# Raw weights of an attention loop on GpSimd's DMA queue, masks on VectorE, partial products in place

## The chip, the cores and the metric

The kernel runs on one core of one Trainium2 chip. The metric is device microseconds of one execution; the time of a kernel is the median of several executions. A core has five engines that run their own instruction streams in order: TensorE (PE, with its weight loads as PEld), VectorE (DVE), ScalarE (ACT), GpSimd (POOL) and SyncE (SP), which here does nothing but issue DMAs. An instruction waits on semaphores for what it needs, and whatever is behind it on its engine waits with it.

## The reference

One inference step of a two-layer encoder trunk, for 512 prompt tokens and 8 x 16 sample tokens (640 tokens, five blocks of 128) that share the weights, all in fp32. Layer 0 is a gated MLP with a spatial mixer; layer 1, where the change lies, is forgetting attention with 16 heads of 128:

```python
proj = h @ w_in                       # (640, 1024) @ (1024, 4 * 2048 + 16): q, k, v, z, forget logits
logf = log_sigmoid(proj[..., 4 * E:] + b_f)
cT = cumsum(logf, axis=1)             # per head
s = einsum('bqhd,bkhd->bhqk', q, k) * scale + cT[..., q] - cT[..., k]
s = where(key_pos <= query_pos, s, -inf)
o = einsum('bhqk,bkhd->bqhd', softmax(s), v)
out = (o * silu(z)) @ w_out
```

Prompt tokens attend to the prompt. Sample tokens attend to 256 cached keys and values of their own sequence (`cache_fox_k`, `cache_fox_v`, `cache_fox_logf`) and to their own 16 new ones. Keys, values and logf of the new tokens are outputs too. After each layer follow a norm, the residual, and a gated embedding.

## The kernel before

**Products with seven multiplications.** fp32 products are made of three fp32r products: each operand is split into a high and a low part (`split`, lines 276 to 283: ACT writes the high part, DVE the low one), and `mm3` (lines 260 to 264) issues high x high, high x low, low x high. In the attention loop a 1024 x 256 panel of `w_in` times the 640 tokens is done in seven block products instead of eight, Strassen-like: `seven_left` yields left operands that are sums and differences of weight blocks, `seven_products` (line 533) multiplies them with sums of token blocks and adds the results up. The weight sums are made by POOL, four additions of 128 x 512 for each panel (`left_operands`, line 203), out of the raw weights into the buffer `SF` (traced as sff). The results' partial sums are `m1`, `u2` and `u3`, three buffers `partial` of 128 x 320 (`HT` = 320 columns, half of the tokens): m1 is written after product 0 (ACT, line 548), u2 after product 1 (DVE, line 550), u3 after product 2 (line 552); they end in the four results `into(i, j)` at products 3 to 6 (line 539, called by `total`).

**Raw weights.** The weights arrive as units of 512 KB; a panel is two units, a pair. From unit `S2` on (64 units, to `S3`) they belong to the attention layer, as in_fox_w_in. `raw_of` says where a unit lies: three slots of 1024 columns (`RAW`), taken in turn. `fetch` issues loads in the order of the units, all on SP's queue through `dma` (line 121). `prefetch` works ahead of TensorE: for each item (a pair's four groups of left operands, j = 0 to 3) it lays down the sums, the split and then `fetch(u + 4)`, at j = 3 `fetch(u + 5)`. With three slots, the second unit of the next pair lies where the first unit of the present one was, so its load waits for POOL's sums and the first split; the unit after that waits for the split of j = 3.

**The attention loop.** Heads go in pairs, p = 0 to 7. In turn p the projections z(p), v(p+1), k(p+1), q(p+1), four panels, are the steps on TensorE (`project`), and `interleave` lays attention pieces of heads 2p and 2p+1 between them, each at a due time in steps' units (a product's k-step counts 0.441, so a panel 12.35). For each prompt head: `setup` splits q and k, and for four query blocks `scores(i)`, `turn(i)` (transposes of the probabilities) and `values(i)`. `scores` first adds the causal mask to the diagonal part of the bias row: w0 is the head's cumulative log-forget row spread over the partitions (`load_w0`, a DMA from c_sc), w1 = w0 + causal for 128 columns (POOL, line 958, one buffer), and DVE subtracts w0 and w1 from the scores while it takes the maximum (lines 968 and 971). For the sample tokens there are two groups of four sequences per pair of heads: `masks` loads the bias `Wc` (from cs_sc) and adds a mask to its last 16 columns (POOL, line 1032) ten units before the scores.

**The queues.** All DMAs of the loop are issued by SP in one order: cached keys (`load_k`, four DMAs each, then turned by DVE at line 1016 out of one buffer), cached values (`load_v`), raw weights, bias rows, stores of new keys (`project_k`: DVE turns them into the buffer `o_vk`, line 904, and 16 DMAs out<-R store them) and of new values, and of y (y_sc). The order of each engine's instructions is planned by a simulation of the program when it is built; the program's order and due times are its input. After the loop, z(7) and the tail of layer 1 follow, in which the last heads' attention lies between the steps of the output product.

Of the kernel before, what the change touches and what calls it, by code (L numbers as in the profile page):

```python
# [20 lines left out]
ALU = mybir.AluOpType  # L21
# [3 lines left out]
P = 128  # L25
# [32 lines left out]
def hybrid_trunk(tc, x_prompt, x_sample, ck, cv, clf, p_prompt, p_sample, norm_pre, norm_post,  # L58
# [58 lines left out]

    behind = {}

    def dma(out, in_):  # L120
        behind["sp"] = nc.sync.dma_start(out=out, in_=in_)  # L121

    @contextmanager
    def queued(*engines):
# [56 lines left out]
    def raw_of(i):  # L181
        if S0 <= i < S1:
            z = (i - S0 + 1) % 4
            if z == NRAW:
                return r1(o_X, 1024)
        else:
            z = i % NRAW if i < S0 else (i + 1) % NRAW
        return RAW[:, z * 1024:z * 1024 + 1024]

    def fetch(upto):  # L190
        while state["raw"] < min(upto, len(units)):
            ap, k = units[state["raw"]]
            dma(raw_of(state["raw"]).rearrange("p (k n) -> p k n", k=k), ap)
            state["raw"] += 1

    def left_operands(i, j):
# [9 lines left out]
    def prefetch(upto, i0=0):  # L206

        while len(place) < min(upto, len(items)):
            i = len(place)
            u, j = items[i]  # L210
            taken = {z for k in range(i0, i) for z in place[k]}
            step = 1 if j == 0 else 2
            free = [z for z in range(0, 2 * (NW - (u in few)), step) if not taken & set(range(z, z + step))]
            if not free:
                return
            z = min(free, key=lambda z: max(last_use[z:z + step]))
            place.append(range(z, z + step))
            last_use[z:z + step] = [i] * step
            fetch(u + 1 if j is None else u + 2)
            o, n = z * 1024, step * 512  # L220
            hi, lo = W[:, o:o + n], W[:, o + n:o + 2 * n]
            if u in joined:
                k = units[u][1]
                hi, lo = (W[:, o:o + 2 * n].rearrange("p (k z n) -> p z k n", z=2, k=k)[:, z] for z in range(2))
                split(hi, lo, raw_of(u).rearrange("p (k n) -> p k n", k=k))
            elif j is None:
                split(hi, lo, raw_of(u))
            else:
                split(*((x.rearrange("p (k n) -> p k n", k=4) for x in (hi, lo)) if j == 0 else (hi, lo)), left_operands(u, j),
                      scale if u in scaled else None)  # L230
                if u > S0:
                    fetch(u + 4 + (u > S1 and j == 3))

    def weights(n):

# [290 lines left out]
        return r1(g // 4 * 2560, 2560).rearrange("p (t n) -> p t n", t=NT)[:, :, (g % 4) * P:(g % 4 + 1) * P]  # L526

    partial = [r1(o_sum + z * HT, HT) for z in range(3)]
    HALF = (slice(0, HT), slice(HT, TOK))

    UZ = (0, 1, 2, 3)

    def seven_products(into, done):

        m1, u2, u3 = partial
        rights = (quarter(0, 0), right_sum(1), quarter(0, 1), right_sum(0), quarter(1, 1), quarter(1, 0), right_sum(2))

        def total(i, j, a, b):
            behind["dve"] = nc.vector.tensor_tensor(out=into(i, j), in0=a, in1=b, op=ALU.add)  # L539
            done(i, j, into(i, j))  # L540

        for n, (w, right) in enumerate(zip(seven_left(), rights)):
            o = bank(UZ)[:, :HT]
            for k in range(4):
                mm3(o, (w[0][:, k], w[1][:, k]), (right[0][:, k], right[1][:, k]), k == 0, k == 3)
                yield 0.441
            if n == 0:
                nc.scalar.activation(out=m1, in_=o, func=AF.Copy)
            elif n == 1:
                nc.vector.tensor_tensor(out=u2, in0=m1, in1=o, op=ALU.add)  # L550
            elif n == 2:
                nc.vector.tensor_tensor(out=u3, in0=u2, in1=o, op=ALU.add)  # L552
            elif n == 3:
                total(1, 1, u3, o)
                nc.vector.tensor_tensor(out=u2, in0=u2, in1=o, op=ALU.add)  # L555
            elif n == 4:
                total(0, 1, u2, o)
            elif n == 5:
                total(0, 0, m1, o)
            else:  # L560
                total(1, 0, u3, o)
# [31 lines left out]
    spatial_loads(1)  # L593
    for g in range(0, 16, 2):
        for part, finish in ((0, finish_u), (1, finish_z)):
            run(seven_products(lambda i, j: uv_of(g + i)[part][:, HALF[j]], lambda i, j, c: finish(g, i, j, c)))
            if part == 0:

                with queued("act", "dve"):
                    spatial_weights(g)  # L600
                    spatial_weights(g + 1)
        if g < 6:

            with queued("act", "dve"):
                layer_norm_panel(1 + g // 2)
        for i in range(2):
            gate_spatial(g + i)
# [139 lines left out]
    SF = pool2.tile([P, 2560], F32, name="sff")  # L747

    o_KT, o_K, o_V, o_q, o_k, o_vk = 0, 2176, 3200, 5248, 6528, 7808
    o_u, o_P, o_PT, o_v, o_qp = 9088, 9728, 10752, 11776, 14336  # L750
    o_Ws, o_Ps, o_PTs, o_W0, o_z = 14848, 15120, 15520, 15904, 16480
    assert o_z + 2 * TOK <= N_R1
    partial = [SF[:, 2048:2048 + HT], r1(o_u, HT), r1(o_u + HT, HT)]


    o = 0
# [163 lines left out]
    def project_z(p):  # L920

        def done(i, j, c):
            th = r1(o_vk + ring("th", (0, 1)) * HT, HT)
            nc.scalar.activation(out=th, in_=c, func=AF.Tanh, scale=0.5)
            nc.vector.scalar_tensor_tensor(out=c, in0=th, scalar=1.0, in1=c, op0=ALU.add, op1=ALU.mult)

        yield from seven_products(lambda i, j: both(o_z, i)[:, HALF[j]], done)

    def project(*parts):
        for part in parts:  # L930
            yield from part

    W0 = [r1(o_W0, 512), tri]
    w1_at = lambda: SF[:, 2368:2368 + P]

    def load_w0(h):
        dma(W0[h % 2], c_sc[h].partition_broadcast(P))

    def prompt_pieces(h):

        p, hh = h // 2, h % 2
        q, k, v = q_of(h), k_of(h), v_of(p)
        w0 = W0[hh]
        zs = (NW - 1) * 2048
        qh, ql, kh, kl = (W[:, zs + z * 512:zs + (z + 1) * 512] for z in range(4))
        O = PB[7]
# [6 lines left out]
        def scores(i):  # L953
            n = (i + 1) * P
            d = slice(i * P, n)
            S = bank(ATT)
            w1 = w1_at()
            nc.gpsimd.tensor_tensor(out=w1, in0=w0[:, d], in1=causal, op=ALU.add)
            if i:
                mm3(S[:, :n], (qh[:, d], ql[:, d]), (kh[:, :n], kl[:, :n]), True, True)  # L960
            else:
                nc.tensor.matmul(S[:, :n], q[:, d], k[:, :n], start=True, stop=True)
            pr = prs[i] = r1(o_P + ring("P", (0, 1)) * 512, 512)
            m = small()
            init = -3e38
            if i:
                m0 = small()
                nc.vector.tensor_tensor_reduce(out=pr[:, :i * P], in0=S[:, :i * P], in1=w0[:, :i * P], scale=1.0, scalar=init,
                                               op0=ALU.subtract, op1=ALU.max, accum_out=m0)
                init = m0  # L970
            nc.vector.tensor_tensor_reduce(out=pr[:, d], in0=S[:, d], in1=w1, scale=1.0, scalar=init,
                                           op0=ALU.subtract, op1=ALU.max, accum_out=m)
            nm, sm = small(), small()
            nc.vector.tensor_scalar(out=nm, in0=m, scalar1=-1.0, scalar2=None, op0=ALU.mult)  # L974
            nc.scalar.activation(out=pr[:, :n], in_=pr[:, :n], func=AF.Exp, bias=nm, accum_out=sm)  # L975
            ri = small()
            nc.vector.reciprocal(out=ri, in_=sm)
            nc.vector.tensor_scalar(out=pr[:, :n], in0=pr[:, :n], scalar1=ri, scalar2=None, op0=ALU.mult)
# [43 lines left out]
    def sample_pieces(p, bg):  # L1022
# [6 lines left out]

        def masks():  # L1030
            dma(Wc, cs_sc[16 * p + 8 * bg:16 * p + 8 * bg + 8].unsqueeze(1).broadcast_to([8, TS, 272]))
            nc.gpsimd.tensor_tensor(out=Wc[:, PAST:], in0=Wc[:, PAST:], in1=CST[:, C_M16:C_M16 + TS], op=ALU.add)

        def scores():
            S = bank(ATT)
            for hh in range(2):
                for bl in range(4):
                    nc.tensor.matmul(S[32 * bl:32 * bl + 32, :272], qpads[:, hh, 4 * bg + bl].rearrange("p h q -> p (h q)"),
                                     kt[:, hh, bl], start=(hh == 0), stop=(hh == 1))
# [71 lines left out]
    def attention_pieces(p, step, s1):  # L1111
# [6 lines left out]
            pieces += prompt_times(2 * p + hh, t0 + 4 * step * hh, step)  # L1118
        if p < 7:
            pieces += [(s0 + 12.1, lambda: load_k(p + 1, 0, 0)), (s1 + 13.5, lambda: load_v(p + 1, 0)),  # L1120
                       (t0 + 4 * step, lambda: load_w0(2 * p + 2))]
        return pieces

    def next_keys(p, t, t_new):
# [4 lines left out]
    sums = []  # L1129

    def sums_of_h():
        sums.append(right_operands((13056, 14336, 15616, o_P, o_V)))

    interleave(project_v0(), [(0.0, forget_logits), (0.1, sums_of_h), (6.0, log_forget)])
    split(*quarter(0, 1), sums[0])
# [15 lines left out]
    pool2.release()  # L1151
    pool2, R2 = second("r2c", F32)
    load_y(range(2, 14))
    w1_at = lambda: r2(9840, P)
    ATT = (5, 6)
    o_junk = r2(9200, 512)
    tail(1, y_again, (0, 1, 2, 3, 4), [(t - now, g) for t, g in pieces if t > now])
# [32 lines left out]
```

## Time and profile before

| | us |
|---|---|
| median of 3 runs (1409.69 to 1413.42) | 1412.28 |
| the profiled execution | 1413.11 |
| its span on the core | 1411.3 |
| busy in it: PE / DVE / ACT / POOL | 1316.6 / 946.7 / 586.6 / 354.9 |

The span runs through layer 0 (its seven-product loop and tail) to about 545 us, the start of layer 1 to about 600, the attention loop from 601 to 1195, and the tail of layer 1. In a row of the profile stand a line of the kernel, an engine, an operation, what it writes and reads by the names of the buffers (R is the large buffer `R1`, A and tbf token operands, W split weights, pb a PSUM bank, SML small columns, CST constants), how often, busy us and the mean ns of one, then the engine's idle time just before them and what ended it. `SPq` is SP's sequencer issuing DMAs. PEclk is the clock that TensorE was granted.

### The profile page before, as it was taken

The numbers are of one execution on the slowest core, as the hardware profiler recorded it, in microseconds if no ns is written. First come the engines' busy times: TensorE is split into PE (matmuls) and PEld (weight loads), VectorE is DVE, ScalarE is ACT, GpSimd is POOL, SyncE is SP. The second block draws the span as 40 slices with busy tenths as digits, with TensorE's granted clock in tenths as the row PEclk, the third lists the DMA queues.
The fourth block names the chain that finished last, engine by engine and source line by source line (L and its number), as shares of the span: only waits on it lengthen the run. The fifth ranks groups of instructions, "written<-read, shape, count | busy, mean of one in ns | idle before, by whom it ended". The sixth has DMA issues, their size and how long they took to land.

```text
span 1411.3 us, 21215 instructions
## 1 busy us (share of the span) xinstructions
PE 1316.6 (93%) x7877; PEld 1169.1 (83%) x7877; DVE 946.7 (67%) x1815; ACT 586.6 (42%) x1061; POOL 354.9 (25%) x332
## 2 busy tenths in 40 slices
PE   9999999999999998999788899798887989999998
PEld 6888999999888887878677798687776978888887
DVE  6745999999434659877556767656665676745553
ACT  4424554445353434343333344333323344545332
POOL 1014444550000003344313334333232332100000
PEclk9999999999999999999899999898998999999999
DMA  6432333323342132577445555576455556743211
GB/s 211 141 99 78 118 123 99 103 81 115 98 153 75 45 110 92 116 136 156 131 114 142 140 121 157 125 152 118 107 131 128 142 122 180 263 153 104 76 53 52
DMA packets 299482, 171.54 MB, mean 122 GB/s; under 512 B 188721, under 2 KB 269409, under 8 KB 299378
## 3 DMA queue, kind: packets, MB, share of 16 engines
q1 hardware_dynamic: 299234, 169.92, 44.5%
q8 instruction: 62, 1.02, 0.3%
q14 instruction: 42, 0.34, 0.1%
q10 hardware_dynamic: 144, 0.26, 0.1%
HBM read 148.55 MB, written 21.59 MB: 121 GB/s over the span
## 4 chain that ended last, share of the span: by engine, by line
PE 64%; DVE 14%; DMA 12%; SPq 4%; issue 4%; ACT 1%; POOL 0%; DVEq 0%; ACTq 0%; POOLq 0%
PE pb L262 19%; PE pb L263 19%; PE pb L264 19%; DMA RAW<-in_fox_w_in 5%; SPq L121 4%; DMA R<-in_cache_fox_k 4%; DVE W L280 3%; DVE R L1016 2%; DMA R<-c_sc 2%; DVE R L539 1%; PE pb L991 1%; DMA R<-in_cache_fox_v 1%; PE pb L571 1%; PE pb L1064 1%; PE pb L306 1%
## 5 line engine op out<-in xcount | busy, mean ns | idle before, releaser
L280 DVE TENSOR_TENSOR W<-RAW,W 128x1024 fp32r<-128x1024 f32 (+1 forms) x140 | 173.4, 1239 | 152.1 <-ACT W L279 150.0
L262 PE MATMUL pb<-A,W 128*128 128x320 f32 x752 | 248.8, 331 | 21.4 <-DVE R L555 21.4
L264 PE MATMUL pb<-A,W 128*128 128x320 f32 x752 | 237.8, 316 | 0.0
L263 PE MATMUL pb<-A,W 128*128 128x320 f32 x752 | 237.8, 316 | 0.0
L279 ACT ACTIVATE W<-RAW 128x1024 fp32r<-128x1024 f32 (+1 forms) x140 | 134.2, 959 | 228.6 <-DMA RAW<-in_fox_w_in 144.7
L262 PE MATMUL pb<-W,A 128*128 128x512 f32 x520 | 204.6, 394 | 1.5 <-ACT A L279 1.5
L263 PE MATMUL pb<-W,A 128*128 128x512 f32 x520 | 203.7, 392 | 0.0
L264 PE MATMUL pb<-W,A 128*128 128x512 f32 x520 | 203.2, 393 | 0.2 <-DVE A L280 0.2
L262 PEld LDWEIGHTS pb<-A,W 128*128 128x128 f32 x752 | 145.7, 194 | 31.0 <-DVE R L555 23.0
L203 POOL TENSOR_TENSOR sff<-RAW 128x512 f32<-128x512 f32 x62 | 84.2, 1359 | 260.6 <-DMA RAW<-in_fox_w_in 188.1
L263 PEld LDWEIGHTS pb<-A,W 128*128 128x128 f32 x752 | 146.0, 194 | 1.7 <-issue 1.3
L264 PEld LDWEIGHTS pb<-A,W 128*128 128x128 f32 x752 | 145.6, 194 | 0.5 <-issue 0.4
L262 PE MATMUL pb<-tbf,W 128*128 128x320 f32 x372 | 126.9, 341 | 18.4 <-DVE R L552 12.8
L264 PE MATMUL pb<-tbf,W 128*128 128x320 f32 x372 | 120.3, 323 | 0.0
L263 PE MATMUL pb<-tbf,W 128*128 128x320 f32 x372 | 120.0, 323 | 0.0
L262 PEld LDWEIGHTS pb<-W,A 128*128 128x128 f32 x520 | 98.1, 189 | 21.0 <-ACT A L279 1.9
L264 PEld LDWEIGHTS pb<-W,A 128*128 128x128 f32 x520 | 98.0, 188 | 20.7 <-DVE A L280 0.7
L263 PEld LDWEIGHTS pb<-W,A 128*128 128x128 f32 x520 | 98.0, 188 | 19.6
L292 POOL TENSOR_TENSOR SML<-SML 128x1 f32<-128x1 f32 x25 | 18.5, 743 | 326.5 <-DVE SML L290 321.8
L262 PEld LDWEIGHTS pb<-tbf,W 128*128 128x128 f32 x372 | 74.8, 201 | 26.7 <-DVE R L552 13.6
L975 ACT ACTIVATE R<-R,SML 128x128 f32<-128x128 f32 (+1 forms) x64 | 35.9, 561 | 115.8 <-DVE SML L974 115.7
L1016 DVE STREAM_TRANSPOSE R<-R 128x256 f32<-128x256 f32 x128 | 47.6, 415 | 45.8 <-DMA R<-in_cache_fox_k 27.7
(256 smaller groups left out, 2800.6 us busy)
## 6 DMA issues: line engine op xcount, KB each, us to landing
RAW<-in_fox_w_in SPq DMA_DIRECT2D x64, 512.0 KB, 7.3
RAW<-in_gmlp_w_in SPq DMA_DIRECT2D x40, 512.0 KB, 3.5
R<-in_cache_fox_v SPq DMA_DIRECT2D x32, 512.0 KB, 7.5
R<-in_cache_fox_k SPq DMA_DIRECT2D x128, 128.0 KB, 5.0
RAW<-in_gmlp_w_out SPq DMA_DIRECT2D x16, 512.0 KB, 3.6
RAW<-in_ple_w_gate SPq DMA_DIRECT2D x16, 512.0 KB, 3.8
RAW<-in_fox_w_out SPq DMA_DIRECT2D x16, 512.0 KB, 4.7
out<-R SPq DMA_DIRECT2D x42, 128.0 KB, 4.7
```

The lines of the kernel that those rows point to most:

```text
L121: behind["sp"] = nc.sync.dma_start(out=out, in_=in_)
L203: nc.gpsimd.tensor_tensor(out=o, in0=a, in1=b, op=op)
L262: nc.tensor.matmul(out, lh, rh, start=start, stop=False)
L263: nc.tensor.matmul(out, lh, rl, start=False, stop=False)
L264: nc.tensor.matmul(out, ll, rh, start=False, stop=stop)
L279: nc.scalar.activation(out=hi, in_=src, func=AF.Copy)
L280: nc.vector.tensor_tensor(out=lo, in0=src, in1=f(hi), op=ALU.subtract)
L292: nc.gpsimd.tensor_tensor(out=q, in0=t, in1=mhalf, op=ALU.pow)
L306: nc.tensor.transpose(out=b[:, j * P:(j + 1) * P], in_=src[:, (4 * c + j) * P:(4 * c + j + 1) * P], identity=ident)
L539: behind["dve"] = nc.vector.tensor_tensor(out=into(i, j), in0=a, in1=b, op=ALU.add)
L975: nc.scalar.activation(out=pr[:, :n], in_=pr[:, :n], func=AF.Exp, bias=nm, accum_out=sm)
L1016: nc.vector.transpose(out=kt[:, hh, bl, :PAST], in_=kraw[:, bl])
```

## The change

It has four parts, all in the attention layer.

1. Loads of raw weights from unit `S2 + 2` to `S3 - 1` are issued on GpSimd's DMA queue (`nc.gpsimd`), not SP's. They use four slots, the fourth being 1024 columns of `R1` (`o_raw`); the last unit takes slot 0. `fetch` is `u + 4` for all items.
2. The causal addition (w1) and the addition of the sample mask are done by DVE; the latter moves from `masks` to the beginning of `scores`.
3. w1 has two buffers, in turn: 128 columns of `R1`, and the constant `blk`. The bias rows w0 of even heads lie in `SF` (where a partial product was) up to head 12, that of head 14 in the fourth slot, for which it is loaded at due time 48 of turn 6 instead of 23.2.
4. `seven_products` uses three of its four results as partial buffers, in place. For z, whose result buffer still holds y of the turn before until it is stored, the partials lie in `o_vk`, with one buffer for the tanh instead of two. That frees the space of the fourth slot.

```diff
-    def dma(out, in_):
-        behind["sp"] = nc.sync.dma_start(out=out, in_=in_)
+    def dma(out, in_, queue=None):
+        if queue is not None:
+            queue.dma_start(out=out, in_=in_)
+        else:
+            behind["sp"] = nc.sync.dma_start(out=out, in_=in_)
...
+        elif S2 + 2 <= i < S3:
+            z = (i - S2) % 4 if i < S3 - 1 else 0
+            if z == NRAW:
+                return r1(o_raw, 1024)
...
-            dma(raw_of(state["raw"]).rearrange("p (k n) -> p k n", k=k), ap)
+            dma(raw_of(state["raw"]).rearrange("p (k n) -> p k n", k=k), ap, nc.gpsimd if S2 + 2 <= state["raw"] < S3 else None)
...
-                    fetch(u + 4 + (u > S1 and j == 3))
+                    fetch(u + 4)
...
-    def seven_products(into, done):
-        m1, u2, u3 = partial
+    def seven_products(into, done, partial=None):
+        m1, u2, u3 = partial or (into(0, 0), into(0, 1), into(1, 0))
...
     def project_z(p):
         def done(i, j, c):
-            th = r1(o_vk + ring("th", (0, 1)) * HT, HT)
+            th = r1(o_vk + 3 * HT, HT)
...
-        yield from seven_products(lambda i, j: both(o_z, i)[:, HALF[j]], done)
+        yield from seven_products(lambda i, j: both(o_z, i)[:, HALF[j]], done, [r1(o_vk + z * HT, HT) for z in range(3)])
...
-    W0 = [r1(o_W0, 512), tri]
-    w1_at = lambda: SF[:, 2368:2368 + P]
+    w1s = r1(o_w1, P), blk
+    def w0_of(h):
+        return tri if h % 2 else SF[:, 2048:2560] if h < 14 else r1(o_raw, 512)
...
-            w1 = w1_at()
-            nc.gpsimd.tensor_tensor(out=w1, in0=w0[:, d], in1=causal, op=ALU.add)
+            w1 = ring("w1", w1s)
+            nc.vector.tensor_tensor(out=w1, in0=w0[:, d], in1=causal, op=ALU.add)
...
         def masks():
             dma(Wc, cs_sc[16 * p + 8 * bg:16 * p + 8 * bg + 8].unsqueeze(1).broadcast_to([8, TS, 272]))
-            nc.gpsimd.tensor_tensor(out=Wc[:, PAST:], in0=Wc[:, PAST:], in1=CST[:, C_M16:C_M16 + TS], op=ALU.add)
         def scores():
             S = bank(ATT)
+            nc.vector.tensor_tensor(out=Wc[:, PAST:], in0=Wc[:, PAST:], in1=CST[:, C_M16:C_M16 + TS], op=ALU.add)
...
-                       (t0 + 4 * step, lambda: load_w0(2 * p + 2))]
+                       (t0 + 4 * step if p < 6 else 48, lambda: load_w0(2 * p + 2))]
```

The rest of the diff lays out `R1` anew, passes `partial` in layer 0's loop (which keeps its three buffers), and gives `sums_of_h` other scratch space.

More of the change, by code (lines that the diff above doesn't have):

```diff
@@ L595, in hybrid_trunk @@
         for part, finish in ((0, finish_u), (1, finish_z)):
-            run(seven_products(lambda i, j: uv_of(g + i)[part][:, HALF[j]], lambda i, j, c: finish(g, i, j, c)))
+            run(seven_products(lambda i, j: uv_of(g + i)[part][:, HALF[j]], lambda i, j, c: finish(g, i, j, c), partial))
             if part == 0:
@@ L749, in hybrid_trunk @@
     o_KT, o_K, o_V, o_q, o_k, o_vk = 0, 2176, 3200, 5248, 6528, 7808
[L750 to L753, printed above, removed]
+    o_P, o_PT, o_v, o_qp = 9088, 10112, 11136, 13696
+    o_Ws, o_Ps, o_PTs, o_w1, o_raw, o_z = 14208, 14480, 14880, 15264, 15456, 16480
+    assert o_w1 + P <= o_raw and o_raw + 1024 <= o_z and o_z + 2 * TOK <= N_R1
     o = 0
@@ L931, in project @@
             yield from part
-    W0 = [r1(o_W0, 512), tri]
-    w1_at = lambda: SF[:, 2368:2368 + P]
+    w1s = r1(o_w1, P), blk
+    def w0_of(h):
+        return tri if h % 2 else SF[:, 2048:2560] if h < 14 else r1(o_raw, 512)
     def load_w0(h):
-        dma(W0[h % 2], c_sc[h].partition_broadcast(P))
+        dma(w0_of(h), c_sc[h].partition_broadcast(P))
     def prompt_pieces(h):
@@ L942, in prompt_pieces @@
         q, k, v = q_of(h), k_of(h), v_of(p)
-        w0 = W0[hh]
+        w0 = w0_of(h)
         zs = (NW - 1) * 2048
@@ L1131, in sums_of_h @@
     def sums_of_h():
-        sums.append(right_operands((13056, 14336, 15616, o_P, o_V)))
+        sums.append(right_operands((o_P, o_v + 1280, o_V, o_qp, o_z)))
     interleave(project_v0(), [(0.0, forget_logits), (0.1, sums_of_h), (6.0, log_forget)])
@@ L1153, in hybrid_trunk @@
     load_y(range(2, 14))
-    w1_at = lambda: r2(9840, P)
     ATT = (5, 6)
```

## The prediction

> **What bounds the kernel now.** I read the profile from the outside in: first the slices and the chain of the page, to see where TensorE is short of its pace; then the busy times of the seven turns of the attention loop; then the waits inside the loop; last, one stall instruction by instruction. The page:
>
> ```profile
> PEclk9999999999999999999899999898998999999999
> ...
> PE pb L262 19%; PE pb L263 19%; PE pb L264 19%; DMA RAW<-in_fox_w_in 5%; SPq L121 4%; DMA R<-in_cache_fox_k 4%; DVE W L280 3%; DVE R L1016 2%; DMA R<-c_sc 2%; DVE R L539 1%; PE pb L991 1%; DMA R<-in_cache_fox_v 1%; PE pb L571 1%; PE pb L1064 1%; PE pb L306 1%
> ```
>
> The granted clock dips only between slices 19 and 30, the attention loop, and the chain that ended last holds three things from that loop that are not arithmetic: landings of the raw weights (in_fox_w_in, 5%), SP's issuing (4%) and landings of cached keys (4%). Next the loop's turns, cut where SP stores y (columns: stretch, its us, busy time with count of PE, weight loads, DVE, ACT, POOL, then clock, DMA share, GB/s):
>
> ```profile
> 601.00:670.00 69.00, 64.46 (x445) 55.70 (x444) 51.83 (x139) 28.66 (x58) 29.33 (x29) 1.00 0.77 147
> 670.00:766.00 96.00, 74.97 (x490) 68.47 (x489) 55.96 (x138) 32.70 (x65) 28.80 (x30) 0.88 0.47 117
> 766.00:845.00 79.00, 72.99 (x521) 66.19 (x520) 57.06 (x138) 32.25 (x65) 29.09 (x30) 0.98 0.59 144
> 845.00:928.00 83.00, 72.58 (x488) 65.83 (x487) 57.09 (x138) 32.14 (x65) 29.04 (x30) 0.92 0.54 135
> 928.00:1014.00 86.00, 76.72 (x533) 70.37 (x532) 56.51 (x138) 32.25 (x65) 28.95 (x30) 0.94 0.63 130
> 1014.00:1109.00 95.00, 74.97 (x483) 67.84 (x482) 56.13 (x138) 32.58 (x65) 28.65 (x30) 0.87 0.48 118
> 1109.00:1195.00 86.00, 79.08 (x557) 73.05 (x555) 60.17 (x145) 35.92 (x71) 28.83 (x30) 0.96 0.61 150
> sum 594.00, PE 515.77 PEld 467.46 DVE 394.74 ACT 226.50 POOL 202.69; mean PE 73.68 PEld 66.78 DVE 56.39 ACT 32.36 POOL 28.96
> ```
>
> Seven turns of nearly the same work take 69 to 96 us, 84.9 on average, and where a turn is long the clock is low (0.87 and 0.88 in the two longest). What is lost against TensorE's own pace: 594.0 - 515.8 = 78 us idle, and the slower clock. The undisturbed third row gives 72.99/521 = 0.140 us for an instruction; the seven counts add to 3517, so 493 us at that pace, 23 us under the 515.8. Together 101 us can be won in the loop by waits alone. No engine is full: DVE is busy 395 of 594 us, POOL 203. So it is the waits:
>
> ```profile
> POOL sff L203 <- DMA RAW<-in_fox_w_in: 173.0, 23, 12.1
> ACT W L279 <- DMA RAW<-in_fox_w_in: 135.8, 20, 11.2
> ...
> DVE W L280 <- ACT W L279: 77.6, 29, 9.3
> POOL R L1032 <- DMA R<-cs_sc: 54.0, 8, 10.1
> ACT W L282 <- DMA RAW<-in_fox_w_in: 46.6, 7, 9.2
> DVE W L283 <- ACT W L282: 42.4, 8, 8.6
> DVE R L1016 <- DMA R<-in_cache_fox_k: 27.7, 6, 10.3
> ...
> DVE R L1016 <- DMA out<-R: 17.9, 3, 7.8
> ```
>
> ```profile
> SPq L121 <- POOL sff L203: 80.6, 14, 7.6
> SPq L121 <- DVE R L1016: 72.1, 25, 7.6
> ```
>
> (us in total, times, longest.) ACT stands 182 us before splits of raw weights that have not landed, DVE behind it 77.6 + 42.4 = 120 us. DVE runs in order, so its sums for the next matmuls stand behind the split. One such stall, from SP, ACT, DVE and PE:
>
> ```profile
> 704.22 6.33 SPq L121 DMA_DIRECT2D R<-in_cache_fox_k  x3
> 710.60 1.51 SPq L121 DMA_DIRECT2D RAW<-in_fox_w_in  x1
> ```
> ```profile
> 719.08 0.63 ACT L282 ACTIVATE W<-RAW 128x512 fp32r<-128x512 f32 x1 [9.16 <-DMA RAW<-in_fox_w_in]
> ```
> ```profile
> 719.74 1.26 DVE L283 SCALAR_TENSOR_TENSOR W<-RAW,W 128x512 fp32r<-128x512 f32 x1 [8.64 <-ACT W L282]
> ```
> ```profile
> 721.93 0.80 PE L962 MATMUL pb<-R 128*128 128x128 f32 x2 [5.61 <-DVE SML L971]
> ```
>
> SP spends 6.33 us issuing three key loads, only then the weights; they land 8 us later, and ACT, DVE and PE stand 9.2, 8.6 and 5.6 us. The loop is bound by the lateness of the weights on SP's one queue: the three slots make SP itself wait (80.6 us for the sums that free a slot), and the key loads wait behind it.
>
> **The change, part by part.** The rows that price it:
>
> ```profile
> L203 POOL TENSOR_TENSOR sff<-RAW 128x512 f32<-128x512 f32 x62 | 84.2, 1359 | 260.6 <-DMA RAW<-in_fox_w_in 188.1
> ```
> ```profile
> RAW<-in_fox_w_in SPq DMA_DIRECT2D x64, 512.0 KB, 7.3
> RAW<-in_gmlp_w_in SPq DMA_DIRECT2D x40, 512.0 KB, 3.5
> ```
> ```profile
> L121 SPq DMA_DIRECT2D R<-in_cache_fox_k  x112: 312/562/6446, 604.5 to 1139.2; - x112
> L121 SPq DMA_DIRECT2D RAW<-in_fox_w_in x52: 367/440/1517, 601.5 to 1142.7; - x52
> ```
> ```profile
> L1048 DVE TENSOR_TENSOR R<-CST,R 128x128 f32<-128x128 f32 x13 | 4.7, 364 | 0.0
> ```
> ```profile
> L1032 POOL TENSOR_TENSOR R<-R,CST 128x16 f32<-128x16 f32 x14 | 3.4, 242 | 48.9 <-DMA R<-cs_sc 48.9
> L958 POOL TENSOR_TENSOR sff<-R,CST 128x128 f32<-128x128 f32 x28 | 21.9, 782 | 45.1 <-DVE SML L971 44.7 <-DMA R<-c_sc 0.3
> ```
>
> *Raw weights over GpSimd's queue, four slots.* 62 loads (32 pairs less the first) leave SP: 62 x 0.44 = 27 us of its issuing, and with them its 80.6 us before L203. On POOL each pair's two loads stand, in the program, behind the four sums of the pair before, and wait for a slot that the split of the last-but-one pair frees; behind them on POOL stand the new keys' copies (L1020) and the next sums. With four slots no load waits for the pair that is being summed. What a load costs POOL is not in this trace, since nothing is issued there. From below: SP's shortest issue of this load, 0.37 us. From above: the longest issue of SP, 6.4 us. I take 1.3 us, one pass of POOL over a quarter of the pair (L203), as the nearest row of that engine. The new circle is then: four sums 4 x 1.36 = 5.4, two issues 2.6, landing 7.3, in all 15.3 us a pair. Today 28 pairs take 594 us, 21.2 each, and TensorE alone needs 493/28 = 17.6. So the circle ends below TensorE, and the even load, which today is issued ahead of the sums and will now be behind them, loses a lead that it has no use for. The landing I leave at 7.3: off SP's queue the weights no longer stand behind key packets (3.5 us in the first layer, without them), but the engines that move both are the same.
>
> What it brings: of the DVE waits that I can name, 120 us come from raw weights and 27.7 + 17.9 = 45.6 from keys and key stores. If TensorE's 101 us go by the same shares, 120/165.6 = 72% or 73 us belong to the weights. Ends: all 101, and half of the 73, if landings stay late.
>
> Against spreading speaks a rule of the Trainium skill (DMA: Bandwidth & Descriptors, "Issuing engines are not separate DMA queues"): transfers of any issuer run on the same 16 engines, and only the time to issue is saved. By it the gain would be the second rival's below. The rows of SP above go against reading it as small here, because what is saved is not 0.44 us of issue but the wait in order behind other loads.
>
> A second rule that speaks against it (SBUF — State Buffer, "Who interferes with whom"): a DMA issued from GpSimd is held up while VectorE runs a one-input operation at double rate. Here those would be the scalings at L978:
>
> ```profile
> L978 DVE TENSOR_SCALAR R<-R,SML 128x128 f32<-128x128 f32 (+3 forms) x56 | 25.8, 461 | 0.8
> ```
>
> If every load met one, the circle would grow by 2 x 0.46 to 16.2 us, still under 17.6; by the rule as by the rows the sum stays as it is. No run before shows it.
>
> *Diagonal masks and sample masks by VectorE.* 64 additions of 128x128 leave POOL (0.78 us each there, in the shade) and come to DVE: 64 x 0.364 = 23.3 us, and 16 of 128x16 at no more than POOL's 0.242 = 3.9. Together 27 us on an engine that is busy two thirds of the loop. Ends: 0 and 27; I take a third, 9 us, as that is about how often DVE was short of time, with TensorE waiting on its sums. The sample mask moves from ten steps ahead to the scores themselves; POOL's 54 us before L1032 go, which held up sums behind it. That I count in the 73.
>
> *Two bias buffers.* POOL no longer writes w1, so its waits for L971 go too. With two buffers the addition need not wait for the last reduction. Nothing counted: the additions are 0.4 us in front of a matmul chain; without that cover each would cost its 0.364, which is the 27 above.
>
> *Partial products in place.* Same instructions; only where they write. For z the three partials lie in the buffer that key stores still read from, and the first is written after one of seven products instead of at the fourth. The only row of such a wait is the 17.9 us of DVE before out<-R, longest 7.8. Ends: 0, and 7 x 7.8 = 55 us if every turn met it; I take 5, since SP, rid of the weights, issues the stores sooner. For v, k and q the earlier write meets readers that are a turn's half behind; 0, or some tenths where a split is late.
>
> *Bias of head 14 in the fourth slot.* It is loaded once, later than now. Ends 0 and one landing of 7.3; I take 2.
>
> **The sum**, against the profiled execution: it took 1413.1 us (span 1411.3), 0.8 over the median 1412.3. -73 + 9 + 5 + 2 = -57, so 1356 by that execution and 1355 by the median. The loop would take 594 - 57 = 537 us, 77 a turn, between the best seen (69) and the next (79). No later stage changes; the next late thing is the key loads, DVE at L1016.
>
> **Rivals.**
> 1. *Descriptors made by POOL are the new bound: slower.* If one issue took more than (21.2 - 5.4 - 7.3)/2 = 4.2 us of POOL, the circle of 5.4 + 2g + 7.3 passes today's 21.2. At 6.4 us, SP's longest, it is 25.5 a pair: 28 x 4.3 = +120, 1533 us. For it: no row of a POOL issue. Against: SP's median is 0.44, and even 3 us would fit under 21.2. Chance 0.10, with 0.03 for smaller losses of the kind.
> 2. *The weights are as late as before for half of the time,* because the landing (7.3 against 3.5 in the first layer) is the shared engines' doing and not the queue's: -36 + 9 + 7 = -20, 1392 us. For it: a DMA share of 0.58 mean in the loop. Against: the two example loads waited 6.3 us on SP before they were issued. Chance 0.16.
> 3. *TensorE takes over:* keys come earlier too, as SP no longer stands 80.6 us; all 101 us go, less DVE's 9: -92, 1320 us. For it: the first turn, 69 us at clock 1.00. Against: key loads use one buffer that a transpose must free (SP's 72.1 us at L1016), and the change leaves that. Chance 0.14.
> 4. *Nothing moves:* the wait for the weights is replaced by one for key stores in place (up to 55 us of DVE, some 34 of TensorE by the share 101/165.6) and DVE's 27 in full: -73 + 61 + 2 = -10, or somewhat less. Chance 0.04 for within 0.3% (4 us, about what this measurement can tell from no change).
>
> **How the numbers follow.** The forecast has the remaining 0.53, 1335 to 1378 by its ends. Faster by over 0.3%: 0.53 + 0.16 + 0.14 = 0.83; within: 0.04; slower: 0.13. The range from 1318 to 1402 takes in rival 2 and most of rival 3.
>
> **What would show it.** In the new profile: 62 loads RAW<-in_fox_w_in from POOL's sequencer, with their duration there (under 2.6 us: right; over 4.2: rival 1). POOL's and ACT's waits for in_fox_w_in fall from 173 and 182 us to under 50 each; if ACT's stays over 90, rival 2. SP's wait for L203 gone in the loop. Half-clock dips fewer, the loop's clock from 0.94 (mean of the seven rows) to 0.97 or more. DVE busy 27 us higher. A wait of ACT at L548 or DVE at L550 for out<-R would be the price of writing in place. The stages before 590 and after 1195 us keep their lengths within 3 us. The prediction fails if POOL's circle is longer than thought, or if the order in which the engines' instructions are laid down, which is planned anew, puts the splits earlier against their loads than now.

## The result, and the profile after

The changed kernel takes 1324.26 us, median of 4 runs (1319.93 to 1325.87); the kernel before took 1412.85 beside it. The ratio is 0.9371, 95% interval 0.9343 to 0.9399: 6.3% faster, 88.6 us. Forecast were 1355 us, with a range of 1318 to 1402 (the forecast's own ends were 1335 and 1378). The profiled execution has a span of 1324.0 us, against 1411.3.

The chain by engine on the page of the kernel before, then the page of the changed kernel, from its parts on busy time, slices, queues and the same chain:

```profile
PE 64%; DVE 14%; DMA 12%; SPq 4%; issue 4%; ACT 1%; POOL 0%; DVEq 0%; ACTq 0%; POOLq 0%
```
```profile
PE 1282.6 (97%) x7877; PEld 1149.1 (87%) x7877; DVE 962.2 (73%) x1895; ACT 589.1 (44%) x1061; POOL 353.9 (27%) x314
...
PEclk8999999999999999978999999999999999999999
...
q1 hardware_dynamic: 266498, 137.41, 37.4%
q0 software_dynamic: 8928, 32.51, 12.6%
...
PE 77%; DVE 11%; DMA 4%; issue 3%; SPq 3%; ACT 1%; POOL 1%; DVEq 0%; POOLq 0%; ACTq 0%
```

DMA's share of the chain that ended last fell from 12% to 4%, and of the four slices of the loop in which the granted clock dipped before, none is low now; a 7 and an 8 stand at 563 to 629 us instead, just ahead of the loop and in its first 28 us. A queue of its own (q0) carries 32.51 MB, 62 x 512 KB. The seven turns, cut again where SP stores y:

```profile
601.00:683.00 82.00, 72.73 (x489) 63.49 (x488) 59.97 (x158) 32.56 (x65) 25.56 (x26) 0.94 0.72 136
683.00:753.50 70.50, 66.49 (x494) 61.75 (x494) 56.77 (x147) 31.20 (x64) 27.28 (x27) 1.00 0.78 159
753.50:822.00 68.50, 68.50 (x513) 64.50 (x513) 58.82 (x150) 33.17 (x66) 29.82 (x29) 1.00 0.70 164
822.00:891.00 69.00, 68.38 (x513) 64.37 (x512) 58.02 (x149) 33.50 (x67) 29.34 (x29) 1.00 0.74 163
891.00:963.50 72.50, 70.26 (x511) 65.55 (x511) 58.86 (x150) 33.07 (x66) 29.40 (x29) 0.98 0.77 155
963.50:1034.50 71.00, 65.14 (x476) 60.42 (x476) 56.04 (x145) 29.97 (x62) 29.59 (x28) 0.98 0.79 159
1034.50:1108.00 73.50, 73.50 (x551) 69.72 (x550) 61.79 (x154) 35.59 (x69) 25.53 (x24) 1.00 0.65 162
sum 507.00, PE 485.01 PEld 449.79 DVE 410.27 ACT 229.07 POOL 196.52; mean PE 69.29 PEld 64.26 DVE 58.61 ACT 32.72 POOL 28.07
```

The loop went from 594 to 507 us, so the 87 us are all there. Its turns, 84.9 us before, take 72.4; after the first they lie between 68.5 and 73.5, where they had spread from 79 to 96. The first turn grew from 69 to 82 us, in part because more work falls before its cut (489 records of TensorE for 445), and at its start VectorE stands 8.8 us before cached keys. TensorE is idle 22 us in the loop (78 before), at a clock of 0.98. Waits inside it, from 601 to 1108 us (us in total, times, longest):

```profile
POOL sff L210 <- DVE W L290: 86.5, 14, 12.2
DVE R L1025 <- DMA R<-in_cache_fox_k: 55.7, 14, 8.8
POOL sff L210 <- DVE SML L986: 50.1, 12, 4.8
POOL sff L210 <- DVE W L287: 44.8, 12, 7.2
...
POOL sff L210 <- DMA R<-in_fox_w_in: 14.1, 3, 5.9
```

POOL's sums (now line 210, and a unit in the fourth slot is R) waited 173 us for landings; now they wait mostly for VectorE, 131 us of it for the splits (L290, L287) that still read the sums made before. ACT's 182 us before raw weights do not appear any more. DVE's wait for keys (now line 1025) doubled, from 27.7 to 55.7 us.

### The profile page after: what moved, and what is told of

The parts are those of the page before. It is cut to its first block, busy times and chain, and to the rows that moved or that the text cites. A ratio compares the mean times of both kernels' runs of the same rounds, so it can differ in the third digit from the quotient of the medians.

```text
span 1324.0 us, 21137 instructions
## 1 busy us (share of the span) xinstructions
PE 1282.6 (97%) x7877; PEld 1149.1 (87%) x7877; DVE 962.2 (73%) x1895; ACT 589.1 (44%) x1061; POOL 353.9 (27%) x314
## 3 DMA queue, kind: packets, MB, share of 16 engines
q1 hardware_dynamic: 266498, 137.41, 37.4%
q0 software_dynamic: 8928, 32.51, 12.6%
## 4 chain that ended last, share of the span: by engine, by line
PE 77%; DVE 11%; DMA 4%; issue 3%; SPq 3%; ACT 1%; POOL 1%; DVEq 0%; POOLq 0%; ACTq 0%
PE pb L269 23%; PE pb L270 23%; PE pb L271 23%; SPq L124 3%; DMA R<-in_cache_fox_k 3%; DVE W L287 2%; PE pb L1000 2%; DVE R L1025 2%; PE pb L1047 1%; PE pb L579 1%; DVE R L987 1%; PE pb L313 1%; PE pb L1073 1%; PE pb L993 1%; DVE W L290 1%
## 5 line engine op out<-in xcount | busy, mean ns | idle before, releaser
L269 PE MATMUL pb<-A,W 128*128 128x320 f32 x752 | 244.6, 325 | 5.1 <-DVE R L547 4.9
L270 PE MATMUL pb<-A,W 128*128 128x320 f32 x752 | 234.5, 312 | 0.0
L271 PE MATMUL pb<-A,W 128*128 128x320 f32 x752 | 234.4, 312 | 0.0
L287 DVE TENSOR_TENSOR W<-RAW,W 128x1024 fp32r<-128x1024 f32 (+1 forms) x125 | 147.8, 1183 | 75.3 <-ACT W L286 73.2
L286 ACT ACTIVATE W<-RAW 128x1024 fp32r<-128x1024 f32 (+1 forms) x125 | 118.6, 949 | 98.8 <-PE pb L271 47.6
L269 PEld LDWEIGHTS pb<-A,W 128*128 128x128 f32 x752 | 143.4, 191 | 13.1 <-issue 6.4
L270 PEld LDWEIGHTS pb<-A,W 128*128 128x128 f32 x752 | 143.1, 190 | 1.2 <-issue 0.9
L271 PEld LDWEIGHTS pb<-A,W 128*128 128x128 f32 x752 | 142.7, 190 | 0.3 <-issue 0.2
L269 PE MATMUL pb<-tbf,W 128*128 128x320 f32 x372 | 123.2, 331 | 9.6 <-ACT tbf L286 4.8
L210 POOL TENSOR_TENSOR sff<-RAW 128x512 f32<-128x512 f32 x47 | 62.9, 1338 | 221.3 <-DVE W L290 78.2
L270 PE MATMUL pb<-tbf,W 128*128 128x320 f32 x372 | 117.7, 316 | 0.0
L271 PE MATMUL pb<-tbf,W 128*128 128x320 f32 x372 | 117.7, 316 | 0.0
L547 DVE TENSOR_TENSOR R<-R,pb 128x320 f32<-128x320 f32 x188 | 88.2, 477 | 21.2 <-PE pb L271 20.4
L1025 DVE STREAM_TRANSPOSE R<-R 128x256 f32<-128x256 f32 x128 | 47.6, 416 | 55.8 <-DMA R<-in_cache_fox_k 55.7
```

What stands on the lines that cost most here:

```text
L210: nc.gpsimd.tensor_tensor(out=o, in0=a, in1=b, op=op)
L269: nc.tensor.matmul(out, lh, rh, start=start, stop=False)
L270: nc.tensor.matmul(out, lh, rl, start=False, stop=False)
L271: nc.tensor.matmul(out, ll, rh, start=False, stop=stop)
L286: nc.scalar.activation(out=hi, in_=src, func=AF.Copy)
L287: nc.vector.tensor_tensor(out=lo, in0=src, in1=f(hi), op=ALU.subtract)
```

## The experiments

The prediction's theory is A: the weights were late because they stood in SP's order behind key loads. Its rivals are B, that the three slots were the cause on any queue, and C, that POOL's masks were. The first six kernels take single parts of the change, or leave one out. Where kernels of different runs are compared, their ratios to the kernel before beside them decide.

**The queue alone.** The kernel before, with one edit:

```diff
-            dma(raw_of(state["raw"])..., ap)
+            dma(raw_of(state["raw"])..., ap, nc.gpsimd if S2 + 2 <= state["raw"] < S3 else None)
```

> The kernel before, with nothing changed but the queue: raw weights of the loop issued by GpSimd, three slots, masks on POOL, three partial buffers. If the loss was the weights' place in SP's order behind key loads (theory A), this alone brings most of the 88 us: 1335 to 1355 us, and ACT's wait for in_fox_w_in falls under 60 us. If it was the three slots (theory B), POOL itself now stands before the load whose slot its sums free, and the sums of the next pair behind it: 1385 to 1415 us. If it was POOL's masks and their single buffer (theory C): 1395 to 1415 us.

Measured: 1429.64 us, ratio 1.0107 (1.0091 to 1.0124). Slower than before. Free of SP's order, with an issue of 0.77 us on an engine that is a quarter busy, the weights are about as late as they were: ACT still stands 125.5 us before them in the loop (182 before) and POOL 135.6 (173). That speaks against theory A. This run alone does not settle it, as POOL's own issuing, some 48 us, could hide a gain; the next one does. POOL in this kernel (start, duration, what; in brackets the idle time before and what ended it):

```profile
687.62 1.29 POOL L206 TENSOR_TENSOR sff<-RAW 128x512 f32<-128x512 f32 x1 [4.05 <-DVE W L283]
688.99 1.62 POOL L206 TENSOR_TENSOR sff<-sff,RAW 128x512 f32<-128x512 f32 x1
690.68 2.16 POOL L206 TENSOR_TENSOR sff<-RAW,sff 128x512 f32<-128x512 f32 x1
692.79 1.52 POOL L122 DMA_DIRECT2D RAW<-in_fox_w_in  x2
694.32 0.47 POOL L961 TENSOR_TENSOR sff<-R,CST 128x128 f32<-128x128 f32 x1
695.23 0.61 POOL L1023 COPY R<-R 128x64 f32<-128x64 f32 x2 [0.43 <-PE pb L1041]
705.02 1.27 POOL L206 TENSOR_TENSOR sff<-RAW 128x512 f32<-128x512 f32 x1 [9.17 <-DMA RAW<-in_fox_w_in]
...
710.21 1.29 POOL L206 TENSOR_TENSOR sff<-RAW 128x512 f32<-128x512 f32 x1
711.58 1.43 POOL L206 TENSOR_TENSOR sff<-sff,RAW 128x512 f32<-128x512 f32 x1
713.09 1.30 POOL L206 TENSOR_TENSOR sff<-RAW,sff 128x512 f32<-128x512 f32 x1
714.33 0.77 POOL L122 DMA_DIRECT2D RAW<-in_fox_w_in  x1
716.63 0.75 POOL L122 DMA_DIRECT2D RAW<-in_fox_w_in  x1 [1.53 <-DVE W L283]
```

This is a circle. Both loads go out when the four sums of the pair before are done (692.79), land together, and the first of the next four sums waits for the later one (705.02); 21.5 us after the first issue comes the next (714.33). The row at 716.63 tells which unit is second: it waits for a split by DVE, that is, for the slot of the unit split last (j = 3), and into that slot goes the *even* unit of the next pair, which all four sums need. The odd one goes into the slot that the sums have just freed. So with three slots the odd load cannot start before the sums end, and the even one not before that split, which here ends 2 us behind them, whatever the queue: 1.5 us of issue, some 10 of landing, 9 to 10 of sums. Other turns of this kernel land sooner, and there a pair takes 18 to 22 us, in this one 23 to 24; the 21.2 us a pair of the kernel before lie in this range.

**All but the queue.** The changed kernel with `None` for `nc.gpsimd`.

> The changed kernel, with the raw weights back on SP's queue: four slots, masks on DVE, two bias buffers, partial products in place. Theory A (SP's order): the loads stand behind key loads as before, 1385 to 1415 us. Theory B (slots): SP no longer waits for POOL's sums, and loads are early enough on any queue: 1325 to 1345 us. Theory C (masks): 1325 to 1350 us.

Measured: 1335.49 us, ratio 0.9436 (0.9418 to 0.9453). Theory B's number: nearly the whole gain with the weights on SP's one queue, so theory A falls. One part of B's expectation missed: SP still stands 67.5 us for the sums. What the queue adds, 9 us by the ratios, is likely in this kernel's waits, from 601 to 1100 us; the changed kernel has none of the first kind below, and 23.2 us of the second, both names of the slots together:

```profile
ACT W L286 <- DMA RAW<-in_fox_w_in: 41.0, 6, 10.5
POOL sff L210 <- DMA RAW<-in_fox_w_in: 39.8, 6, 8.6
```
```profile
SPq L124 <- POOL sff L210: 67.5, 16, 8.6
```

**All but the masks' move.** `masks` and the causal addition on `nc.gpsimd` as before, on top of the change.

> The changed kernel, with both mask additions back on POOL and the sample mask back in its early place; queue, slots, two bias buffers and partial products as changed. Theory A: within 8 us of the changed kernel, 1316 to 1332 us (DVE is relieved of 25 us, POOL's loads stand behind waits for bias rows now and then). Theory C: POOL's sums and now its loads stand behind the masks' waits again: 1345 to 1390 us.

Measured: 1337.16 us, ratio 0.9461 (0.9438 to 0.9484), 13 us over the changed kernel. Neither theory's number: A and B had 1316 to 1332, C 1345 or more. POOL now waits before the sample mask, with sums and loads behind it (from 601 to 1100 us):

```profile
POOL R L1041 <- DMA R<-cs_sc: 80.9, 14, 8.4
```

**The masks' move alone.** The kernel before, with both additions by `nc.vector`.

> The kernel before, with both mask additions on DVE and the sample mask in the scores; one bias buffer, three slots, SP's queue. Theories A and B: 1408 to 1425 us (25 us more of DVE's time, a third of it on the path, POOL's 54 us before the sample mask gone). Theory C: 1340 to 1390 us.

Measured: 1410.2 us, ratio 0.9961 (0.9946 to 0.9977). Theory C falls too as the main cause: in the three-slot circle the masks matter little.

**All but the fourth slot.**

```diff
-        elif S2 + 2 <= i < S3:
-            z = (i - S2) % 4 if i < S3 - 1 else 0
-            if z == NRAW:
-                return r1(o_raw, 1024)
...
-                    fetch(u + 4)
+                    fetch(u + 4 + (u > S1 and j == 3))
```

> The changed kernel, with three slots and the fetches of before; GpSimd's queue, DVE's masks, two bias buffers and partial products in place stay. New theory (circle): with three slots both loads of a pair go out behind the sums that free their slots, land together, and the next sums wait for both, so a pair takes two issues, some 9 us of landing and 9 to 10 us of sums, 21 us or so: 28 x (21.5 - 17.6) slower, 1400 to 1440 us, and POOL's wait for in_fox_w_in is back over 100 us. Rival (the rest of the change does it, the slot only with the queue): under 1370 us.

Measured: 1410.99 us, ratio 0.9953 (0.993 to 0.9975). Take the slot away and 6% are gone. POOL and ACT wait again, from 601 to 1100 us:

```profile
POOL sff L206 <- DMA RAW<-in_fox_w_in: 169.0, 20, 11.1
ACT W L282 <- DMA RAW<-in_fox_w_in: 93.7, 16, 10.4
```

**The fourth slot alone.** The changed kernel with SP's queue, both masks on POOL, one bias buffer. Partial products in place and the moved bias rows stay, as they make the room.

> The kernel before with the fourth slot alone and what makes room for it (partial products in place, bias rows moved): SP's queue, masks on POOL, one bias buffer. Circle theory: the even load of a pair has a pair's lead and only the odd one stands between two pairs' sums; most of the gain is here, 1335 to 1365 us. Rival (the parts are worth something only together): 1380 to 1415 us.

Measured: 1343.17 us, ratio 0.9482 (0.946 to 0.9505): by the ratios 73 us of 89. Theory B is right in both directions: without the slot the rest gains next to nothing, and the slot with what makes room for it gains most. What four slots do, in the changed kernel's POOL rows:

```profile
684.00 1.63 POOL L210 TENSOR_TENSOR sff<-RAW,sff 128x512 f32<-128x512 f32 x1
685.57 0.77 POOL L122 DMA_DIRECT2D RAW<-in_fox_w_in  x1
687.01 0.75 POOL L122 DMA_DIRECT2D R<-in_fox_w_in  x1 [0.67 <-DVE W L287]
...
692.64 1.29 POOL L210 TENSOR_TENSOR sff<-RAW 128x512 f32<-128x512 f32 x1 [2.41 <-DVE SML L1052]
698.64 1.30 POOL L210 TENSOR_TENSOR sff<-RAW,R 128x512 f32<-128x512 f32 x1 [4.71 <-DMA R<-in_fox_w_in]
700.01 1.30 POOL L210 TENSOR_TENSOR sff<-sff,RAW 128x512 f32<-128x512 f32 x1
701.40 1.27 POOL L210 TENSOR_TENSOR sff<-R,sff 128x512 f32<-128x512 f32 x1
702.61 0.77 POOL L122 DMA_DIRECT2D RAW<-in_fox_w_in  x1
```

Two loads still go out behind the sums, but they are other units. The second, waiting for DVE's split, is now the odd one (R, the fourth slot, holds only odd units). The first goes into the slot that the sums have just freed, and that is now the even unit of the pair after next: the loads into R, units 19, 23, 27 and on, come one place later in the order of issue than their numbers, as an even unit goes before each. So the even unit has a pair's lead, the first sum (692.64) runs before the odd one lands, and only three sums stand behind the landing (698.64). From 687.01 to the end of the sums at 702.67 are 15.7 us, less than TensorE's 17.6 us a pair.

**Twice the issues.** Each raw load issued by POOL as two of 256 KB.

> The changed kernel, each raw load of the loop issued by POOL as two of 256 KB: POOL's issuing doubles from 62 x 0.77 = 48 to about 95 us. If POOL's issuing has room (TensorE sets the pace): 1322 to 1334 us. If POOL's circle sets it, each pair loses 1.5 us: 1360 to 1370 us.

Measured: 1325.09 us, ratio 0.9355 (0.9334 to 0.9375), no loss. An issue of half the size takes POOL about the same time:

```profile
L122 POOL DMA_DIRECT2D RAW<-in_fox_w_in x78: 722/724/733, 620.8 to 1074.5; - x78
```

So 62 more issues, 45 us of POOL, change nothing: there is room in its circle, and the prediction's first rival was far off.

**Another queue of SP's kind.** The raw loads by `nc.scalar`.

> The changed kernel, the raw loads issued by ACT: a queue apart from SP's, but of SP's kind, and not in POOL's order. If what the queue adds (1335 to 1324 us) is being apart from SP's key loads: 1318 to 1332 us. If it is GpSimd's own way of moving (4 KB packets, 8,928 of them for 32.5 MB): 1332 to 1345 us. ACT's splits and exponentials stand behind loads that wait for a slot, which could cost more: up to 1360 us.

Measured: 1323.6 us, ratio 0.9343 (0.9326 to 0.9361). What the queue adds is being apart from SP's other loads; that it is GpSimd's is worth nothing. On ACT an issue takes half of POOL's time, the second row being the changed kernel's:

```profile
L122 ACTq DMA_DIRECT2D RAW<-in_fox_w_in x39: 374/375/408, 618.4 to 1069.3; - x39
```
```profile
L122 POOL DMA_DIRECT2D RAW<-in_fox_w_in x39: 748/766/775, 624.5 to 1072.7; - x39
```

**The causal addition alone back on POOL.** Only the line of w1 is `nc.gpsimd` again.

> The changed kernel, with the causal addition alone back on POOL (two bias buffers); the sample mask stays on DVE. With both on POOL it took 1337 us, and POOL waited 81 us for the rows of the sample mask. If that wait is what the masks' move saves: 1321 to 1328 us here. If the causal additions in POOL's order are: 1332 to 1340 us.

Measured: 1333.64 us, ratio 0.9411 (0.9395 to 0.9426). The time lies in the second range. By the ratios (0.9411 and 0.9461 against 0.9371) the causal additions are some 6 of the masks' 13 us, about half, and this kernel's interval just touches that of the changed one; the rest would be the sample mask and the wait for its rows. In this kernel, from 601 to 1100 us, POOL stands before them for DVE, two buffers or not, and they take it 0.46 to 1.03 us each in the mean of their forms:

```profile
POOL CST L967 <- DVE SML L980: 39.5, 20, 5.8
```

That the sums and loads behind this wait are how it reaches TensorE is only argued.

**Late sample masks, and late keys.** Three tries at what is left. The first makes the load of the sample mask's rows due later, `(t0 - 4, masks)` for `(t0 - 10, masks)`; the second does so with the raw loads on ACT; the third issues the key loads by `nc.scalar`, raw loads on POOL.

> The changed kernel, the load of the sample mask's rows due 4 steps ahead of the scores, not 10. SP stands 86 us in the loop before that load, since its one buffer is still read, and key loads stand behind it. If late keys (DVE waits 56 us for them) still cost TensorE time: 1312 to 1321 us. If TensorE sets the pace: within 4 us of 1324.

> Both: raw loads issued by ACT, and the sample mask's rows loaded late. If keys are what is late: 1310 to 1320 us. If TensorE sets the pace: 1319 to 1327 us.

> The changed kernel, the key loads issued by ACT, so that they stand behind nothing of SP's. 128 issues of some 0.5 us are 64 us of ACT's time, and ACT's splits stand behind each that waits for the keys' buffer. If SP's order makes the keys late: 1312 to 1320 us. If the keys' one buffer does: 1324 to 1345 us, with ACT waiting in SP's place.

Measured: 1325.89 us (ratio 0.9361, 0.9347 to 0.9375), 1320.47 us (0.9323, 0.9309 to 0.9338) and 1346.5 us (0.9499, 0.9468 to 0.9529). The first changes nothing, DVE's wait for keys included: 55.5 us. The second is the fastest seen, 0.4% under late masks alone beside it; against the raw loads on ACT without it the intervals overlap. The third lies just above its second range, with runs from 1336 to 1351 us. In it DVE's wait for keys falls to 17.4 us, but it then waits 28.7 us for ACT's splits (4.6 in the changed kernel, both from 601 to 1100 us); that ACT now stands in its order for the keys' one buffer, as SP did, is the likely reason and was not tried apart. Late keys thus seem to cost little by now: TensorE is idle for 22 us of the loop in all.

## Why the prediction was right, and where it was not

*What bound the loop.* Right that the loss of 101 us lay in the loop, came from raw weights by way of ACT's splits and DVE's order, and could nearly all be won: 87 went. Wrong was the step that named the cause, "the loop is bound by the lateness of the weights on SP's one queue". The queue alone made the kernel 1.1% slower, the slot with what makes room for it 5.2% faster. The stall chosen as the example misled, though it was no exception: in nearly every turn two weight loads stand behind three key loads each on SP, 2.5 to 6.7 us at a time. (The rows showed one such load; the second rival's "two example loads" is a slip.) But off SP's queue a pair took as long, as its loads still had to wait for their slots. Nor was SP's longest wait, 80.6 us for the sums, the loss: with four slots on SP's queue it is still 67.5 us, at nearly the whole gain.

*The circle.* Its size for the new kernel was about right (15.3 forecast, 15.7 measured in one pair), by luck, as its errors cancelled: one issue of 0.75 us counts, not two of 1.3 each; 10.9 us and not 7.3 pass from its end to the next sum, which waits for the landing; and three sums, 4.0 us in all, stand behind it, not four, 5.4 in all, since one runs ahead. The same sum was not made for the kernel before. With the prediction's prices (two issues of 0.44, 7.3, 5.4) it would have come to 13.6 us and missed the 21.2; with the lengths of the trace, some 10 us of landing and 9 to 10 of sums, it comes to about 21, and none of its members goes by the queue, which the run of the queue alone bears out.

*The term of the weights.* -73 forecast, for the queue and the slot together; all of the change but the masks' move gives -76 by its ratio (0.9461), and the slot with what makes room for it -73 (0.9482). The size was right, but it was derived from shares of waits and laid to the queue; that it fits is partly luck. The rest of the change, another 16 us, is more than its parts: from the slot alone, the queue with the second bias buffer adds 3 us (0.9482 to 0.9461, not clear of noise), and the masks' move with that buffer 6 or 7 (0.9482 to 0.9436).

*The masks.* Forecast as 9 us lost; 13 us won (1337.2 against 1324.3; by the ratios, 0.9461 against 0.9371). The additions take DVE 22.6 us in the loop (L967 and L1044), near the 27 priced, and its busy time there rose by 15.5; but TensorE's waits for DVE fell there from 68 to 16 us. What I put at nothing, POOL's causal additions "in the shade", was the wrong term: they stand in one order with sums and loads. POOL's wait for the sample mask's rows had been counted in the 73.

*In place, and the bias of head 14.* 7 us were put down. No wait of ACT's or DVE's for out<-R is left in the changed kernel's loop, DVE's 17.9 us before (line 1016) included, and the kernel with three slots, which has both, is no slower than the kernel before (0.9953); so the price is near 0 by the waits; neither part was run alone.

*The second rule*, of DMAs held up by VectorE (the Trainium skill, SBUF — State Buffer, "Who interferes with whom"): no sign here. POOL's issues in the rows above take 748 to 775 ns, and a queue of SP's kind gives the same time. The first rule, that spreading over issuers saves only the time to issue (the Trainium skill, DMA: Bandwidth & Descriptors, "Issuing engines are not separate DMA queues"), was nearer the truth than my reading of SP's rows: alone the queue gained nothing, and with four slots and the masks on DVE 9 us (0.9436 to 0.9371), which the run with ACT's queue puts down to being apart from SP's other loads.

*The rivals.* The third, TensorE takes over at 1320 us with a chance of 0.14, came within 5 us, though the keys did not come earlier as it supposed. The measured 1324 us lie below the forecast's own ends, 1335 to 1378, and inside the range only because that takes in this rival: the sum was 31 us too high, and 22 of them are the masks, forecast at +9 and measured at -13.

## What to carry to other kernels

When an engine waits for a load, write down the whole circle from one load to the next through the buffer that it needs: who frees the buffer, who issues, how long it lands, who reads first. If the circle's length is the period that the profile shows, look for another buffer or a shorter member before another queue: here the queue alone changed nothing, and the buffer nearly everything. Before a part of a change is credited, ask what the circle would be with that part alone.

## What the runs showed that was not expected

VectorE's scaling of probabilities (L978 before, L987 after) got slower with the same code, most at 384 columns; the first row is the kernel before, the second the changed one, the third the one with the raw loads on ACT:

```profile
L978 DVE TENSOR_SCALAR R<-R,SML 128x384 f32<-128x384 f32 x14 | 5.7, 405 | 0.3
```
```profile
L987 DVE TENSOR_SCALAR R<-R,SML 128x384 f32<-128x384 f32 x14 | 12.5, 891 | 0.2
```
```profile
L987 DVE TENSOR_SCALAR R<-R,SML 128x384 f32<-128x384 f32 x14 | 12.5, 893 | 0.2
```

It is the same where POOL issues no DMA, so it is not the issuing. The trace of the changed kernel shows what it is: all 14 instances of 128x384 in the loop fall into two kinds, by which of the two engines began first. Two of each engine:

```profile
710.31 1.30 POOL L210 TENSOR_TENSOR sff<-RAW 128x512 f32<-128x512 f32 x1 [3.51 <-DVE SML L986]
740.77 1.48 POOL L210 TENSOR_TENSOR sff<-sff,RAW 128x512 f32<-128x512 f32 x1
```
```profile
710.33 1.49 DVE L987 TENSOR_SCALAR R<-R,SML 128x384 f32<-128x384 f32 x1
740.72 0.38 DVE L987 TENSOR_SCALAR R<-R,SML 128x384 f32<-128x384 f32 x1
```

Six that begin 0.02 to 0.03 us behind a sum of POOL take 1.48 to 1.49 us, about the sum's 1.3 and some more, and a seventh, 0.63 us behind one, 0.88. The other seven take 0.38 to 0.41: they begin just ahead of a sum, in the last 0.2 us of one, or with none beside them. In the kernel before all 14 are of this second kind. So a scaling that begins while a sum is under way ends only after it, and the new order of instructions put it there; why the two engines hold each other up, no run here shows.

GpSimd's queue moved the 32.51 MB in 8,928 packets, 3.6 KB each. On SP's queue the same loads took about 1 KB a packet: q1 has 299,234 packets before and 266,498 after, 32,736 fewer for 62 loads of 512 KB.
